# Separate accumulator banks at the projection's end, an early first step for the MLP's second product, and later due times for its weights

## The chip, the cores and the metric

The kernel runs on one core of one Trainium2 chip. The engines of the core are TensorE (PE in the rows; its weight loads are PEld), VectorE (DVE), ScalarE (ACT), GpSimd (POOL) and SyncE (SP), which only issues transfers here; ACT issues some too. The metric is the device time in microseconds (us), lower is better.

## The reference

One decoder layer over 1024 prompt tokens and 64 sample tokens: a mixing sub-layer (differential attention and sparse attention, in parallel, one output projection) and a squared-ReLU MLP, both with an RMS norm before and after.

```python
mix = jnp.concatenate([o_diff, o_nsa], axis=-1) @ w_out     # 1024 x 1024
x = x + rms_norm(mix, g_post_mix)
hm = rms_norm(x, g_pre_mlp)
ff = jnp.square(jax.nn.relu(hm @ w_up)) @ w_down            # 1024 x 4096, 4096 x 1024
x = x + rms_norm(ff, g_post_mlp)
```

Everything is fp32.

## The kernel before

Each fp32 operand is split into a high and a low part: ACT copies the high part (L139), DVE subtracts to get the low part (L1364). Three matmuls (high x high, low x high, high x low) make one fp32 product, so before PE can use a new operand it needs one ACT and one DVE instruction on it.

Four stages matter here, and they follow one another without a barrier. The program order is handed to a scheduler that works out its own time line and so decides the order on each engine; then each engine runs its rows strictly in that order, and waits where a row's input is not there.

1. **Attention.** Its last work items (score, transpose T, product o) end while the projection begins.
2. **Projection** (`phase_out`). The weights of `w_out` are loaded and split (`weight(k)`, 8 of them), and for each of nine token tiles `front(t)` loads the attention's output and splits it, `prod(t, 0)` and `prod(t, 1)` make two half rows (C, 24 matmuls of 512 columns each), and `post(t)` does norm, residual, second norm and transposes (T, 8 of them). `post` is a chain over engines: ACT (sum of squares), DVE, POOL (`rstd`), DVE (L1309, L1310), ACT, DVE, POOL, DVE (L1314), then the transposes on PE. C has 3 of the 8 accumulator banks, T has 2. `x_factor` (DVE, ACT) then builds the token side of the MLP's operands; `up_open` and `up_factor` load and build its first weight side.
3. **MLP up** (`phase_up`). One level of a seven-product scheme for a 2x2 block product (`UORD`, `DORD` give the order of the products), tiled over 16 column blocks j. The tokens are two quarters p (`QT` = 272 columns). For j = 0 the first quarter is done alone, `products(0, (0,))`, while the operands of the second quarter are still being built; then its second quarter, then the other j. The accumulators Ua to Ud take two banks each, all eight, so they can be opened only when C and T are done with theirs. Results (uh) go to hF in DRAM by SP.
4. **MLP down** (`phase_down`). 128 steps n over (product i, row block sb): each step needs a 128-row block of a quarter of `w_down` (wf, from q or qe) and a row block of hF (hf, from hr), both split by ACT and DVE; the first 96 issue 24 matmuls of 272 columns each (Dn, L1648), the last 32 half of that (L1658). The 16 steps of the first product use quarter 0 alone; its first eight blocks come in two 1 MB loads on ACT's queue into qe, the other eight into q02 and q03 on SP's. The chunks of quarters 1, 3 and 2 (q10 to q23, 1 MB each) are loaded later: a gate, a copy of one element on DVE (L1552) at step `gate` = 2, 6, 10, ..., holds each load back; DVE then combines the chunk with another one (L1566, L1568). `finish` writes result rows; `fin` gives it one of four rooms.

## Time and profile before

| what | value |
|---|---|
| three runs | 1845.38, 1856.58, 1858.5 us; median 1856.58 |
| profiled execution, its own time | 1848.67 us |
| its span | 1846.9 us (1.8 us lie around it) |
| PE busy | 1718.9 us, 93% of the span |
| projection | about 973 to 1098 us |
| MLP up | about 1107 to 1456 us |
| MLP down | about 1469 to 1834 us, then the last rows until 1846.9 |

Times in the rows are us from the start of the span. The granted clock of PE (PEclk) is a share of full speed, averaged over the stretch. Matmuls are pipelined and their ends are modelled, so a row's duration is a little more than the time until the next row.

### The profile page before, as it was taken

What the parts mean: (1) busy time and instruction counts of PE and PEld (TensorE: products, weight loads), DVE (VectorE), ACT (ScalarE), POOL (GpSimd) and SP (SyncE); (2) the same over time, 40 slices, a digit from 0 to 9 for tenths busy, and PEclk for the clock granted to TensorE, in tenths of its full rate; (3) what the DMA queues carried; (4) which work ended last, traced back from release to release, by engine and by line L of the source; (5) the groups of instructions that cost most, each with busy time, mean ns of one, the idle gap of its engine ahead of it and who ended that gap; (6) DMA issues with size and microseconds to landing.
All of it is one profiled execution on the core that took longest, in us unless ns stands there. A gap on an engine that the chain in (4) does not pass through costs nothing.

```text
span 1846.9 us, 33392 instructions
## 1 busy us (share of the span) xinstructions
PE 1718.9 (93%) x12155; PEld 1494.1 (81%) x12155; DVE 1137.5 (62%) x2713; ACT 867.2 (47%) x2188; POOL 275.8 (15%) x517
## 2 busy tenths in 40 slices
PE   7698999999998999999978978999999689999997
PEld 7677776676656877788867858999999689999996
DVE  5357657667753666667583477665766356747655
ACT  5254446556652554546462345444444234443442
POOL 2134325333320111111110010000000000000000
PEclk9888999999998999999988989999999889999999
DMA  7521000001104342433253322443443545544434
GB/s 204 111 72 43 13 11 21 7 7 42 35 8 135 107 123 67 139 89 118 74 198 100 116 84 71 138 153 138 143 145 114 213 163 171 177 119 116 114 118 140
DMA packets 193904, 191.92 MB, mean 104 GB/s; under 512 B 32547, under 2 KB 152971, under 8 KB 193739
## 3 DMA queue, kind: packets, MB, share of 16 engines
q1 hardware_dynamic: 190810, 184.30, 32.5%
q10 hardware_dynamic: 2928, 5.48, 0.9%
q8 instruction: 96, 1.57, 0.4%
q14 instruction: 70, 0.57, 0.1%
HBM read 133.75 MB, written 55.97 MB: 103 GB/s over the span
## 4 chain that ended last, share of the span: by engine, by line
PE 76%; DVE 8%; DMA 6%; issue 3%; ACT 2%; SPq 1%; POOL 1%; ACTq 0%; DVEq 0%; POOLq 0%
PE Dn L1648 12%; PE M L337 11%; PE S L410 5%; PE o L502 5%; PE Uc L1438 5%; PE Ua L1438 5%; PE Ub L1438 5%; PE T L517 4%; PE C L1294 4%; PE Dn L1658 3%; PE Ud L1438 2%; DMA q<-w_down 2%; PE o L614 2%; PE S L1097 1%; PE o L1222 1%
## 5 line engine op out<-in xcount | busy, mean ns | idle before, releaser
L1648 PE MATMUL Dn<-hf,wf 128*128 128x272 f32 x2304 | 296.7, 292 | 22.9 <-ACT hf L139 13.7
L1648 PEld LDWEIGHTS Dn<-hf,wf 128*128 128x128 f32 x2304 | 295.1, 192 | 24.4 <-ACT hf L139 14.1
L337 PE MATMUL M<-w,xt 128*128 128x384 f32 (+4 forms) x1584 | 296.1, 332 | 13.2 <-ACT natk L139 10.7
L337 PEld LDWEIGHTS M<-w,xt 128*128 128x128 f32 (+1 forms) x1584 | 246.0, 192 | 28.5 <-ACT natk L139 11.5
L427 ACT ACTIVATE p<-S,nm 128x512 f32<-128x512 f32 (+3 forms) x288 | 160.2, 562 | 87.4 <-DVE nm L422 47.2
L175 POOL TENSOR_TENSOR rs_r<-rs_t,mhalf 128x1 f32<-128x1 f32 (+2 forms) x64 | 39.7, 621 | 983.1 <-DVE rs_t L173 980.1
L418 DVE TENSOR_REDUCE nm<-S 128x1 f32<-128x512 f32 (+3 forms) x288 | 148.2, 528 | 58.0 <-PE S L417 37.8
L410 PE MATMUL S<-kst,qs 128*128 128x512 f32 (+3 forms) x576 | 162.5, 373 | 9.0 <-ACT p L427 8.2
L481 POOL TENSOR_SCALAR p<-p,coef 128x640 f32<-128x640 f32 (+7 forms) x128 | 92.9, 739 | 150.2 <-DVE coef L478 66.3
L410 PEld LDWEIGHTS S<-kst,qs 128*128 128x128 f32 x576 | 94.1, 194 | 22.1 <-ACT p L427 11.4
L1364 DVE TENSOR_TENSOR us<-ur,us 128x512 fp32r<-128x512 f32 x96 | 65.9, 691 | 66.5 <-ACT us L139 66.5
L1438 PE MATMUL Ub<-xc,us 128*128 128x272 f32 x768 | 105.7, 290 | 0.8 <-ACT us L139 0.8
L1438 PE MATMUL Ua<-xc,us 128*128 128x272 f32 x768 | 103.4, 290 | 2.3 <-ACT uh L139 2.3
L139 ACT ACTIVATE wf<-q 128x512 fp32r<-128x512 f32 x72 | 45.7, 635 | 125.9 <-PE Dn L1648 118.4
L139 ACT ACTIVATE us<-ur 128x512 fp32r<-128x512 f32 x101 | 63.3, 629 | 83.3 <-PE Uc L1438 50.2
L1438 PEld LDWEIGHTS Ua<-xc,us 128*128 128x128 f32 x768 | 99.6, 190 | 2.6 <-ACT uh L139 2.5
L1438 PEld LDWEIGHTS Ub<-xc,us 128*128 128x128 f32 x768 | 100.6, 190 | 1.1 <-ACT us L139 1.0
L150 DVE COPY pt<-T 128x512 f32<-128x512 f32 (+3 forms) x100 | 61.8, 619 | 55.3 <-PE T L517 41.5
L139 ACT ACTIVATE hf<-hr 128x544 fp32r<-128x544 f32 (+1 forms) x128 | 75.6, 591 | 43.0 <-PE Dn L1658 29.2
L1364 DVE TENSOR_TENSOR hf<-hr,hf 128x544 fp32r<-128x544 f32 (+1 forms) x128 | 82.7, 649 | 19.8 <-ACT hf L139 19.6
L139 ACT ACTIVATE pt<-T 128x512 f32<-128x512 f32 (+4 forms) x116 | 60.8, 527 | 68.9 <-PE T L517 41.1
L1364 DVE TENSOR_TENSOR wf<-q,wf 128x512 fp32r<-128x512 f32 x72 | 49.8, 691 | 69.7 <-ACT wf L139 69.7
(340 smaller groups left out, 3336.9 us busy)
## 6 DMA issues: line engine op xcount, KB each, us to landing
hF<-uh SPq DMA_DIRECT2D x105, 272.0 KB
hr<-hF SPq DMA_DIRECT2D x92, 272.0 KB
kvp<-cache_diff_kv SPq DMA_DIRECT2D x128, 128.0 KB
ur<-w_up SPq DMA_DIRECT2D x32, 512.0 KB
q<-w_down SPq DMA_DIRECT2D x14, 1024.0 KB
raw<-w_in SPq DMA_DIRECT2D x32, 192.0 KB
raw<-w_in SPq DMA_DIRECT2D x40, 128.0 KB
hr<-hF SPq DMA_DIRECT2D x32, 136.0 KB
```

The source lines that it names most:

```text
L139: self.nc.scalar.activation(out, in_, AF.Copy, scale=scale)
L337: nc.tensor.matmul(ps[1][:m, :n], self.xt[c][:, a, k, c0:c0 + m], ws[k][:, b, :n], start=i == 0, stop=i == len(ops) - 1)
L410: nc.tensor.matmul(S[:, a * P - lo:b * P - lo], qs[:, ps, j, :], kst[hf][:, kc, a * P - lo:b * P - lo], start=ps == 0, stop=ps == 1 and no ...
L418: nc.vector.reduce_max(nm[:, n:n + 1], S[:, a * P - lo:b * P - lo], axis=AX.X, negate=True)
L427: nc.scalar.activation(p[:, a * P:b * P], tiles[n][:, a * P - lo:b * P - lo], AF.Exp, bias=nm[:, 0:1], accum_out=sums[:, n:n + 1])
L481: nc.gpsimd.tensor_scalar(v, v, coef[:, sw + 1, j:j + 1], 0.0, op0=OP.mult, op1=OP.add)
L502: nc.tensor.matmul(st["o"][half * 64:half * 64 + 64, pr * 256:pr * 256 + 256], lhsT, rhs, start=not started[half], stop=last, skip_group_c ...
L517: nc.tensor.transpose(T[:, m * 256 + jj * P:m * 256 + jj * P + P], st["p", sw, pr * 2 + jj][:, kb * P:(kb + 1) * P], self.ident)
L1294: nc.tensor.matmul(ps[:m], mhs[t][:, a, k, :m], ws[k][n][:, b], start=cnt == 0, stop=cnt == 3 * KC - 1)
L1364: lo.tensor_sub(w[:, 1], src, f32(w[:, 0]))
L1438: nc.tensor.matmul(ps[:, p, :QT], w[:, a, k, :], x[:, b, k, :], start=start and cnt == 0, stop=cnt == 11, skip_group_check=True)
L1648: nc.tensor.matmul(dps[db][:, q, :QT], w[:, a, db * P:(db + 1) * P], h[:, b, q * QT:(q + 1) * QT], start=st and m == 0, stop=sp and m == 2)
```

## The change

In `phase_out`, `front(0)` stands ahead of all weights, and the opening of the MLP's first weights stands between tile 7 and tile 8 of the second half rows. The first quarter of j = 0 gets banks of its own, one each (Va to Vd, pool `psU0`), open from the start of the projection; T keeps one bank, and U is opened when the first quarter is done. `down_open` loads block 0 of `w_down`'s quarter 0 (eq) and row block 0 of the first product of hF (eh0) while MLP up runs. The rest of quarter 0 is cut into blocks 1 to 4 and 5 to 8 (qe, ACT's queue), 9 to 12 (q03) and 13 to 15 (q04, both SP). The gates of the later chunks stand at 6, 10, 14, ... in place of 2, 6, 10, ...; `fin` has three rooms; uh has 12 buffers, not 13, and some pools lie elsewhere.

```diff
@@ -1265,10 +1265,8 @@
             nc.vector.tensor_sub(mh[:, 1, :, :m], mx[:, :, :m], f32(mh[:, 0, :, :m]))
             pss[t] = []
 
-        for k in range(2):
-            weight(k)
         front(0)
-        for k in range(2, KC):
+        for k in range(KC):
             weight(k)
         for i in UORD[:5]:
             self.xtile(self.xca, i, 0)
...
@@ -1343,12 +1341,13 @@
         for t in range(NT - 1, NT + 1):
             front(t)
             prod(t, 0)
-        self.up_open()
-        for i in UORD[:5]:
-            self.up_factor(0, i)
         for t in range(NT - 1, NT + 1):
             prod(t, 1)
             post(t)
+            if t < NT:
+                self.up_open()
+                for i in UORD[:5]:
+                    self.up_factor(0, i)
...
@@ -1439,15 +1438,16 @@
...
-        def products(j, pq, nxt, st=lambda: self.sp.tile([P, 2, QT], F32, name="uh", bufs=13)):
...
             def ptile(x):
-                if pq[0] == 0:
-                    self.ups[x] = psU.tile([P, 2, 512], F32, name=f"U{x}", tag=f"U{x}")
-                t = self.ups[x]
+                if pq == (0,):
+                    t = self.psU0.tile([P, 1, 512], F32, name=f"V{x}", tag=f"V{x}")
+                else:
+                    t = self.psU.tile([P, 2, 512], F32, name=f"U{x}", tag=f"U{x}")
                 return t, t[:, s, :QT]
...
         turn = iter(UORD)
-        products(0, (0,), lambda i: self.x_factor(next(turn), 1), lambda: self.sp.tile([P, 1, QT], F32, name="uh", bufs=13))
+        products(0, (0,), lambda i: self.x_factor(next(turn), 1), lambda: self.sp.tile([P, 1, QT], F32, name="uh", bufs=12))
         close(1)
         for j in range(NJ):
             if j + 2 < NJ:
                 load(j + 2)
+            if j == NJ - 2:
+                self.down_open()
             products(j, (0, 1) if j else (1,), lambda i: factor(j + 1, i))
+
+    def down_open(self):
+
+        nc = self.nc
+        self.eq = self.early.tile([P, 1, 512], F32, name="eq")
+        nc.sync.dma_start(self.eq, self.A["w_down"][0].rearrange("(s e p) c -> e p s c", e=2, p=P)[0, :, 0:1, 0:512])
+        self.eh = []
+        for sb in range(1):
+            h = self.early.tile([P, HT], F32, name=f"eh{sb}")
+            nc.sync.dma_start(h, self.hF[DORD[0], sb * P:sb * P + P])
+            self.eh.append(h)
...
         def load_w(q, c, gate=None):
-            early = q == 0 and c < 2
-            t = quarter[q, c] = (qe if early else qp).tile([P, 4, 512], F32, name="qe" if early else f"q{q}{c}",
-                                                           bufs=2 if early else 1)
+
+            r, e = q % 2, q // 2
+            s0, s1 = (max(c * 4 - 3, 0), min(c * 4 + 1, NB)) if q == 0 else (c * 4, c * 4 + 4)
+            if q == 0 and c == 0:
+                t = self.eq
+            elif q == 0 and c < 3:
+                t = qe.tile([P, 4, 512], F32, name="qe", bufs=2)
+            else:
+                t = qp.tile([P, s1 - s0, 512], F32, name=f"q{q}{c}")
             if gate is not None:
                 nc.vector.tensor_copy(t[:, 0, 0:1], gate)
-            r, e = q % 2, q // 2
-            (nc.scalar if early else nc.sync).dma_start(t, w_dn[e, :, c * 4:c * 4 + 4, r * 512:r * 512 + 512])
+            for sb in range(s0, s1):
+                quarter[q, sb] = t[:, sb - s0]
+            if (q, c) != (0, 0):
+                (nc.scalar if q == 0 and c < 3 else nc.sync).dma_start(t, w_dn[e, :, s0:s1, r * 512:r * 512 + 512])
 
 
         def factor(n):
             if n >= len(hr):
                 return
             i, sb, p = hr[n]
-            load_h(n + HB)
-            a11, a21, a12, a22 = ((quarter[q, sb // 4][:, sb % 4] if (q, sb // 4) in quarter else None)
-                                  for q in range(4))
+            load_h(n + 4)
+            a11, a21, a12, a22 = (quarter.get((q, sb)) for q in range(4))
...
         def fin(n):
 
-            if n < 4:
-                room[n] = None
-            if room[n % 4] is None or n >= 4:
-                room[n % 4] = qe.tile([P, 4, 512], F32, name="qe", bufs=2) if n % 4 < 2 else \
-                    qp.tile([P, 4, 512], F32, name=f"q0{n % 4}")
-            return room[n % 4]
-
-        room = {}
+            return qp.tile([P, 4, 512], F32, name="q03") if n % 3 == 2 else qe.tile([P, 4, 512], F32, name="qe", bufs=2)
+
         gate = {}
         for k, (q, c) in enumerate([(q, c) for q in (1, 3, 2) for c in range(4)]):
-            gate[2 + (k % 4) * 4 + (k // 4) * NB] = (q, c)
-        for c in range(4):
+            gate[6 + (k % 4) * 4 + (k // 4) * NB] = (q, c)
+        R.update(enumerate(self.eh))
+        for c in range(5):
             load_w(0, c)
-            load_h(c, nc.scalar)
             if c < 2:
+                load_h(2 * c + 1, nc.scalar)
+                if c:
+                    load_h(2, nc.scalar)
                 factor(c)
...
                 self.rr = e(self.pool("rr", side="right"))
+                self.wa = e(self.pool("wa", side="right"))
                 xca = e(self.pool("xca", side="right"))
-                self.wa = e(self.pool("wa"))
...
+                up0 = e(ExitStack())
+                self.psU0 = up0.enter_context(self.pool("psU0", psum=True))
                 with self.pool("w2", 11) as self.wp, self.pool("cl") as cl, \
-                        self.pool("psC", 3, psum=True) as self.psC, self.pool("psT2", 2, psum=True) as self.psT:
+                        self.pool("psC", 3, psum=True) as self.psC, self.pool("psT2", 1, psum=True) as self.psT:
...
-                with self.pool("xcb") as xcb, self.pool("psU", psum=True) as psU:
+                early = ExitStack()
+                self.early = early.enter_context(self.pool("early"))
+                with self.pool("xcb") as xcb, ExitStack() as ps:
...
                         self.xstack[0].close()
                         if p == 1:
                             self.xstack[1].close()
+                            up0.close()
+                            self.psU = ps.enter_context(self.pool("psU", psum=True))
                         self.sp = self.xstack[0].enter_context(self.pool(f"sp{p}", side="right"))
...
+            with early, self.pool("qe", side="right") as qe, self.pool("fd") as fp, self.pool("qd") as qp, \
                     self.pool("psDn", 4, psum=True) as psD:
                 self.phase_down(qe, qp, fp, psD)
```

Three places show what this does to the order of rows. The first is PE at the end of attention (T, o) and the projection's start (C, by weights `w` and `us`). Before:

```order
L1294 MATMUL C_12910<-w_12847,xm_12815 128x512 x3
L1294 MATMUL C_12910<-w_12855,xm_12815 128x512 x3
L1294 MATMUL C_12910<-w_12863,xm_12815 128x512 x3
L1294 MATMUL C_12971<-us_12799,xm_12968 128x512
L603 MATMUL T_12728<-ident_64,p_12675 128x128 [waits Activation_49]
L603 MATMUL T_12728<-ident_64,p_12675 128x128 x3
L614 MATMUL o_12735<-vst_11344,pt_12726 128x128 [waits Activation_49]
L614 MATMUL o_12735<-vst_11344,pt_12726 128x128 x3
L1294 MATMUL C_12971<-us_12799,xm_12968 128x512 x2
L1294 MATMUL C_12971<-us_12807,xm_12968 128x512 x3
L1294 MATMUL C_12971<-us_12820,xm_12968 128x512 x3
L1294 MATMUL C_12971<-us_12828,xm_12968 128x512 x3
```

and with the change:

```order
L565 MATMUL T_12710<-ident_64,jk_12702 128x128 [waits DVE_49,PE_49]
L603 MATMUL T_12721<-ident_64,p_12675 128x128 [waits PE_49]
L603 MATMUL T_12721<-ident_64,p_12675 128x128 x3
L603 MATMUL T_12728<-ident_64,p_12675 128x128 [waits Activation_49]
L603 MATMUL T_12728<-ident_64,p_12675 128x128 x3
L614 MATMUL o_12735<-vst_11344,pt_12726 128x128 [waits Activation_49]
L614 MATMUL o_12735<-vst_11344,pt_12726 128x128 x3
L614 MATMUL o_12735<-vst_11345,pt_12733 128x128 [waits Activation_49]
L614 MATMUL o_12735<-vst_11345,pt_12733 128x128 x2
L614 MATMUL o_12735<-vst_11345,pt_12733 128x128 [waits Pool_49]
L565 MATMUL T_12754<-ident_64,jk_12746 128x128 [waits DVE_49,PE_49]
L1292 MATMUL C_12886<-us_12807,xm_12802 128x512 x3
```

Before, the last transposes and o products of attention stand between C matmuls of two tiles (72 C matmuls ahead of the last T); now all of attention is first and C follows it.

The second is PE at the projection's end; the last C rows are tile 8's second half, T_13702 are its transposes. Before:

```order
L1294 MATMUL C_13658<-w_12863,xm_13545 64x512 x3
L1319 MATMUL T_13646<-ident_64,ctmp_13627 128x128 [waits DVE_49,Activation_49]
L1319 MATMUL T_13646<-ident_64,ctmp_13627 128x128 x3
L1319 MATMUL T_13652<-ident_64,ctmp_13627 128x128 [waits Activation_49]
L1319 MATMUL T_13652<-ident_64,ctmp_13627 128x128 x3
L1319 MATMUL T_13702<-ident_64,ctmp_13683 128x64 [waits DVE_49,Activation_49]
L1319 MATMUL T_13702<-ident_64,ctmp_13683 128x64 x3
L1319 MATMUL T_13709<-ident_64,ctmp_13683 128x64 [waits Activation_49]
L1319 MATMUL T_13709<-ident_64,ctmp_13683 128x64 x3
L1438 MATMUL Ua_13751<-xc00_12866,us_13583 128x272 x12
L1438 MATMUL Ub_13768<-xc50_12867,us_13586 128x272 [waits PE_49,Activation_49]
```

and with the change (T_13503 belongs to tile 6, C_13661 is the second half of tile 8):

```order
L1437 MATMUL Va_13754<-xc00_12869,us_13642 128x272
L1317 MATMUL T_13503<-ident_64,ctmp_13478 128x128 [waits Activation_49]
L1317 MATMUL T_13503<-ident_64,ctmp_13478 128x128 x3
L1437 MATMUL Va_13754<-xc00_12869,us_13642 128x272 x6
L1437 MATMUL Vb_13771<-xc50_12870,us_13645 128x272 [waits Activation_49]
L1437 MATMUL Vb_13771<-xc50_12870,us_13645 128x272 x3
L1437 MATMUL Vb_13771<-xc50_12870,us_13645 128x272 [waits DVE_49]
L1437 MATMUL Vb_13771<-xc50_12870,us_13645 128x272 x7
L1437 MATMUL Vc_13822<-xc40_12873,us_13658 128x272 [waits Activation_49]
L1437 MATMUL Vc_13822<-xc40_12873,us_13658 128x272 x3
L1292 MATMUL C_13661<-w_12810,xm_13548 64x512 [waits DVE_49]
L1292 MATMUL C_13661<-w_12810,xm_13548 64x512 x2
```

Va, Vb and the beginning of Vc now stand ahead of the last 24 C matmuls; the transposes of tiles 7 and 8 follow after them and eight more matmuls of Vc, and Vd follows the transposes.

The third is the change from MLP up to MLP down, on ACT (L1554 and L1574 are loads of weights, L1545 and L1557 those of hF; L1462 and L1463 are MLP up's last squared ReLU). Before:

```order
L1463 ACTIVATE uh_17450<-uh_17450 128x544 [waits Activation_49]
L1554 DMA qe_17568<-w_down 128x4x512 [waits DMAHW7_49,PE_49]
L1554 DMA qe_17580<-w_down 128x4x512 [waits DMAHW0_49]
L1462 ACTIVATE uh_17396<-uh_17396 128x544 [waits DMAHW6_49,DMAHW2_49,DVE_49]
L1463 ACTIVATE uh_17396<-uh_17396 128x544 [waits Activation_49]
L139 ACTIVATE wf_17574<-qe_17568 128x512 [waits DMAHW7_49]
L139 ACTIVATE wf_17586<-qe_17568 128x512
L139 ACTIVATE wf_17608<-qe_17568 128x512
L1545 DMA hr_17570<-hF_60 128x544 [waits DMAHW5_49]
```

and with the change:

```order
L139 ACTIVATE wf_17587<-eq_17123 128x512
L139 ACTIVATE hf_17590<-eh0_17125 128x544
L1463 ACTIVATE uh_17465<-uh_17465 128x544 [waits Activation_49]
L1574 DMA qe_17593<-w_down 128x4x512 [waits DMAHW0_49]
L1574 DMA qe_17607<-w_down 128x4x512 [waits DMAHW1_49]
L1462 ACTIVATE uh_17411<-uh_17411 128x544 [waits DMAHW5_49,DMAHW2_49,DVE_49]
L1463 ACTIVATE uh_17411<-uh_17411 128x544 [waits Activation_49]
L139 ACTIVATE wf_17601<-qe_17593 128x512 [waits DMAHW0_49]
L139 ACTIVATE wf_17621<-qe_17593 128x512
L139 ACTIVATE wf_17657<-qe_17593 128x512 [waits PE_49]
L1557 DMA hr_17583<-hF_60 128x544 [waits DMAHW7_49]
```

The splits of step 0 (wf from eq, hf from eh0) now stand ahead of the two loads of qe; step 1's hF load stands where step 0's stood. On DVE, the gate of q10 and its first use, before (wf and hf are the splits of steps 0 to 3):

```order
L1364 TENSOR_TENSOR wf_17608<-qe_17568,wf_17608 128x512 [waits Activation_49]
L1552 COPY q10_17674<-wf_17608 128x1 [waits DVE_49]
L1364 TENSOR_TENSOR hf_17577<-hr_17570,hf_17577 128x544 [waits DMAHW5_49,Activation_49]
L1364 TENSOR_TENSOR hf_17589<-hr_17582,hf_17589 128x544 [waits DMAHW0_49,Activation_49]
L1364 TENSOR_TENSOR wf_17644<-qe_17568,wf_17644 128x512 [waits Activation_49]
L1566 TENSOR_TENSOR qe_17568<-qe_17568,q10_17674 128x512 [waits DMAHW4_49,DVE_49]
L1566 TENSOR_TENSOR qe_17568<-qe_17568,q10_17674 128x512 x2
L1566 TENSOR_TENSOR qe_17568<-qe_17568,q10_17674 128x512 [waits DVE_49]
```

and with the change (splits of steps 6 to 8):

```order
L1363 TENSOR_TENSOR hf_17756<-hr_17619,hf_17756 128x544 [waits DMAHW7_49,Activation_49]
L1570 COPY q10_17815<-wf_17753 128x1 [waits DMAHW5_49,DVE_49]
L1363 TENSOR_TENSOR wf_17785<-qe_17607,wf_17785 128x512 [waits Activation_49]
L1363 TENSOR_TENSOR hf_17788<-hr_17655,hf_17788 128x544 [waits DMAHW0_49,Activation_49]
L1363 TENSOR_TENSOR wf_17820<-qe_17607,wf_17820 128x512 [waits Activation_49]
L1363 TENSOR_TENSOR hf_17823<-hr_17687,hf_17823 128x544 [waits DMAHW1_49,Activation_49]
L1585 TENSOR_TENSOR eq_17123<-eq_17123,q10_17815 128x512 [waits DMAHW4_49,DVE_49]
L1585 TENSOR_TENSOR qe_17593<-qe_17593,q10_17815 128x512 x3
```

The gate's copy and the subtraction moved from steps 0 and 2 to steps 6 and 8; two steps lie between them in both.

## Rows read from the trace of the kernel before

**Rows 1.** The page: busy time of PE, and the chain that ended last
```profile
PE 1718.9 (93%) x12155; PEld 1494.1 (81%) x12155; DVE 1137.5 (62%) x2713; ACT 867.2 (47%) x2188; POOL 275.8 (15%) x517
...
PE 76%; DVE 8%; DMA 6%; issue 3%; ACT 2%; SPq 1%; POOL 1%; ACTq 0%; DVEq 0%; POOLq 0%
```

**Rows 2.** Stretches: length, busy us and instructions by engine, PEclk, DMA share, GB/s
```profile
960.00:980.00 20.00, 16.83 (x72) 13.55 (x71) 11.29 (x26) 10.33 (x29) 2.21 (x2) 0.77 0.58 183
980.00:1000.00 20.00, 14.85 (x74) 11.99 (x73) 4.68 (x8) 5.32 (x15) 1.10 (x2) 0.92 0.27 86
1080.00:1100.00 20.00, 14.44 (x59) 9.28 (x58) 13.60 (x22) 8.76 (x18) 1.46 (x3) 0.83 0.23 78
1100.00:1120.00 20.00, 13.62 (x89) 13.54 (x90) 17.00 (x19) 10.33 (x18) 0.72 (x2) 0.74 0.09 22
...
1460.00:1480.00 20.00, 9.83 (x56) 9.61 (x56) 6.07 (x10) 5.43 (x10) 0.00 (x0) 0.66 1.04 382
```

**Rows 3.** PE in order of time at the switch: start, us, what, [idle before, releaser]
```profile
1454.83 1.66 PE L1438 MATMUL Uc<-xm,us 128*128 128x272 f32 x12
1468.90 8.79 PE L1648 MATMUL Dn<-hf,wf 128*128 128x272 f32 x48 [12.41 <-ACT hf L139]
1478.95 1.27 PE L1648 MATMUL Dn<-hf,wf 128*128 128x272 f32 x8 [1.27 <-ACT hf L139]
1486.88 5.37 PE L1648 MATMUL Dn<-hf,wf 128*128 128x272 f32 x24 [6.66 <-DVE hf L1364]
...
1504.73 25.47 PE L1648 MATMUL Dn<-hf,wf 128*128 128x272 f32 x202
```

**Rows 4.** ACT in order of time at the switch (ACTq: issue of transfers)
```profile
1456.53 1.00 ACTq L1554 DMA_DIRECT2D qe<-w_down  x2
...
1462.00 0.63 ACT L139 ACTIVATE wf<-qe 128x512 fp32r<-128x512 f32 x1 [3.00 <-DMA qe<-w_down]
1462.01 0.35 ACTq L1545 DMA_DIRECT2D hr<-hF  x1
...
1468.19 0.66 ACT L139 ACTIVATE hf<-hr 128x544 fp32r<-128x544 f32 x1 [4.52 <-DMA hr<-hF]
```

**Rows 5.** SP and DVE in order of time at the switch
```profile
1467.97 1.19 SPq L1554 DMA_DIRECT2D q<-w_down  x2
...
1483.09 2.50 DVE L1566 TENSOR_TENSOR qe<-qe,q 128x512 f32<-128x512 f32 x4 [7.01 <-DMA q<-w_down]
```

**Rows 6.** MLP down: who waited for whom (total, times, longest), and PE's row
```profile
DVE q L1568 <- DMA q<-w_down: 8.1, 3, 3.6
...
1575.36 14.91 PE L1648 MATMUL Dn<-hf,wf 128*128 128x272 f32 x102 [1.75 <-DVE wf L1364]
```

**Rows 7.** PE in order of time inside and at the end of the projection
```profile
1046.83 7.86 PE L1294 MATMUL C<-w,xm 128*128 128x512 f32 x33
...
1090.14 8.27 PE L1294 MATMUL C<-w,xm 128*64 128x512 f32 x24 [4.84 <-DVE ctmp L1309]
1098.25 1.03 PE L1319 MATMUL T<-ident,ctmp 128*128 128x128 f32 x8
1106.38 1.08 PE L1319 MATMUL T<-ident,ctmp 64*128 64x64 f32 x8 [7.09 <-DVE ctmp L1314]
1107.39 3.09 PE L1438 MATMUL Ua<-xc,us 128*128 128x272 f32 x12
```

**Rows 8.** The stretch after the projection: columns as in the second group
```profile
1106.00:1128.00 22.00, 17.85 (x116) 17.04 (x116) 21.18 (x25) 13.90 (x22) 0.00 (x0) 0.85 0.04 13
```

**Rows 9.** PE in order of time at the projection's start
```profile
972.83 3.75 PE L1294 MATMUL C<-us,xm 128*128 128x512 f32 x15
...
994.20 0.30 PE L565 MATMUL T<-ident,jk 128*128 128x128 f32 x1 [1.55 <-DVE jk L563]
998.10 6.20 PE L1294 MATMUL C<-w,xm 128*128 128x512 f32 x15 [3.60 <-DVE ctmp L1309]
```

**Rows 10.** C's matmuls alone in the same stretch: length, PE, PEld, PEclk, DMA share, GB/s
```profile
972.00:994.20 22.20, 17.79 (x72) 13.23 (x72) 0.98 0.15 48
```

**Rows 11.** The last stretch: columns as in the second group
```profile
1834.00:1847.00 13.00, 0.39 (x4) 0.11 (x2) 7.43 (x9) 3.10 (x6) 2.52 (x3) 0.72 0.24 91
```

More of the change, by code (lines that the diff above doesn't have):

```diff
@@ L1424, in up_open, with phase_up @@
         load(1)
-    def phase_up(self, psU, close):
+    def phase_up(self, close):
         nc = self.nc
```

5 lines of the change are left out of this document (2 added, 3 removed).

## Prediction

> **What bounds the kernel now.** The page first: PE is busy 93% of the span and makes 76% of the chain that ended last [rows 1]. So PE sets the time, and a change can only give back time in which PE stands still or runs slowly. The table of stretches shows where that is: the reader is to look at PE's busy column and at PEclk together. Three places stand out [rows 2]: the projection's start (16.83 and 14.85 of 20 us busy), its end (14.44 and 13.62, clock 0.83 and 0.74), and the switch from MLP up to MLP down (9.83, clock 0.66). They are the three places that the change touches. For each, PE's rows in order of time give the wait and what ended it. A change within 1% (18.6 us) is about what a measurement of this kernel can't tell from no change.
>
> **The switch from MLP up to MLP down.** The last Uc matmuls end at 1454.83 + 1.66 = 1456.49; the first Dn starts at 1468.90 after 12.41 us [rows 3]. ACT's rows show why: the loads of qe are issued at 1456.53, the first lands 5.5 us later at 1462.00, only behind it does ACT's queue issue step 0's hF load (1462.01), and that lands 6.2 us later at 1468.19 [rows 4]. Then 48 matmuls take 8.79 us, 1.27 us of waiting, 8 matmuls, another wait of 6.66, and 24 matmuls in 5.37, until 1492.25 [rows 3]. Dense, 202 matmuls take 25.47, so 0.126 each and 3.03 a step [rows 3]. By 1492.25 there are 80 done, worth 10.1 us; 35.8 have gone by, so 25.7 are lost. The second wait comes from DVE: its in-order queue held q10's subtraction for 7.01 us, since q10 was issued after 1467.97 and landed only at 1483.09, 15 us later, with the transfer engines full (DMA share 1.04, 382 GB/s) [rows 2, 5].
>
> With the change, step 0's operands are on the chip before MLP up ends, and its splits stand ahead of the last ones of MLP up. They are two instructions of about 0.7 on ACT and two on DVE [rows 4], ahead of the last additions and under the last Uc matmuls. So step 0 follows Uc directly and dense: 1456.5 to 1459.5. Step 1 then hangs on the chain on which step 0 hung: qe, then an hF load behind it on ACT's queue. With the same two latencies it starts at 1468.9, so PE waits 9.4. Its clock will have fallen, as it had after the 12.41 before: I take the same 48 matmuls in 8.79, 2.7 over dense. After that nothing holds DVE, because q10's gate and subtraction stand at steps 6 and 8, when the first quarter's traffic is through. Two steps, 6.1 us, lie between them, as for all twelve chunks before and after; three of these already made DVE wait 8.1 in all at L1568, for which PE paid 1.75 in the largest case [rows 6]. I allow 1 us for q10. Lost: 9.4 + 2.7 + 1 = 13.1, against 25.7: **a gain of 12.5**. The upper bound is 15, if step 1's load lands at once after qe's two (DVE and PE then start some 2 us earlier). The lower bound is 8: by 1463 the new order has asked for (by the tiles' shapes) 2.1 MB of qe, 1.8 of q03 and q04, three hF loads of 0.28, the norm's 0.5 and MLP up's last four stores, 1.1; these 6.3 MB at 382 GB/s [rows 2] take 16.5, so if step 1's load is the last of them it lands near 1473 in place of 1468.2, and 4 to 5 of the gain are gone. The Trainium skill, page "DMA: Bandwidth & Descriptors", section "Issuing engines are not separate DMA queues", says that transfers of ACT, SP and GpSimd run on the same 16 engines and interleave, so a second queue gives no priority. By that rule the sum would stand nearer to 8 than to 12.5; the trace doesn't contradict it, as 6.2 us for 272 KB are long. I keep 12.5, because step 0's load before had much the same company and took those 6.2.
>
> The other eleven gates come four steps later, with unchanged distance to their use, and all are needed at the earliest 16 steps after the chunk they replace. So mid-down I count nothing, with 4 us each way for where the stalls of [rows 6] fall. Three rooms in place of four touch only the last tiles, which end behind DVE and ACT work [rows 11]; the third room's earlier store has ended by then: 0, at most +1.
>
> **The projection's end.** PE waits 4.84 for a C bank (DVE's L1309), runs tile 8's 24 matmuls in 8.27, waits 7.09 for post(8)'s chain, and starts U at 1107.39 [rows 7]. Dense, 33 C matmuls take 7.86 [rows 7], so 24 take 5.7: the low clock cost 2.6. That is 14.5 in all. With own banks, Va, Vb and Vc fill these waits. But they only move PE's work forward. The work behind is DVE's: the token operands of both quarters and the first weights, in one queue with post's steps. DVE is busy 21.18 of the 22 us behind the projection [rows 8], and the second quarter of j = 0 can't start until it is through, whatever PE did meanwhile; U's banks overlie V's, so it waits for the first quarter's readers as well. PE can gain only what DVE was idle for: 6.4 in 1080 to 1100 and 3.0 in 1100 to 1120 [rows 2], 9.4 at most, and most of that is post's alternation of ACT, DVE and POOL, which stays; the transposes of tile 8 now even queue behind C and V on PE. The other bound: thinly spread PE work runs at the low clock for one more tile, a loss of 2.6. I take **a gain of 2**, nearer to the lower end, as the row nearest to it, DVE's 21.18 of 22, shows that engine full.
>
> The single T bank makes each tile's transposes two halves with an eviction between. 24 C matmuls (5.7 us) lie around them and hide it in tiles 0 to 6; if that cover were gone, half a transpose group (0.5 us) a tile would show. Counted at nothing.
>
> **The projection's start.** Before, C begins at 972.83, and its matmuls fill the waits of attention's tail, up to the last transpose at 994.20; then PE waits 3.60 for post(0) [rows 9]. C's 72 matmuls take 17.79 of those 22.2 us [rows 10]. With the change attention's tail runs alone and C follows it without a break. Without C in between, the tail can be faster: PE's own work in it is 22.2 - 17.8 = 4.4, and its ACT and DVE links (splits and transposes of two heads) come to about as much again, so C begins some 8 later, near 981. The 72 matmuls then take 72 x 0.238 = 17.1 dense, until 998.1, just where the next C matmul started before: the 3.60 for post(0) is covered, since two tiles' halves lie between. The weights' splits behind front(0) cost nothing as long as attention's tail covers them; without that cover the 16 low parts would show on DVE, 0.7 each. After the thin tail the first tile runs at the low clock, 2.6 as above for 24 matmuls. I take **a loss of 2**. Bounds: -4, if the tail needs only its 4.4 and C ends its 72 near 994.3; +13.5, if the last transpose comes at 994.20 as before and all 17.1 of C lie behind it, less the 3.6.
>
> **Sum.** -12.5 - 2 + 2 = -12.5. The profiled execution took 1848.67, so its like would be 1836.2. The median of the three runs lies 7.9 above the profile, and nothing says which level the next runs take; I put the change on the median: 1856.6 - 12.5 = **1844**.
>
> **Rivals.**
> *The projection's end is freed.* If DVE's queue can take post(7) and post(8) earlier because V's products let it start their evictions early, all of 9.4 and 2.6 come back in place of 2: 10 more, 1834. For it speak DVE's idle 9.4, against it DVE's 21.18 of 22.
> *The loads interleave.* Step 1's load shares its engines with all that is asked for at once: the gain at the switch is 8 or less, the sum -8, 1848.5; if q10 then still holds DVE, only the early step 3.03 remains, and the sum is -3, 1853.5. DMA share 1.04 speaks for it, the earlier load's 6.2 us against it.
> *Attention's tail lies open, and the kernel is slower.* C is the filler of 960 to 1000. If the tail's links take as long without it as with it, the last transpose again comes near 994, PE loses 13.5 in place of 2, and its first tile runs at the low clock (2.6): 1844 - 2 + 13.5 + 2.6 = 1858. It decides when the last transpose comes later than about 992. Against it: before, PE's queue itself delayed that chain, with up to 18 C matmuls between two of its links.
>
> **Chances.** My forecast 0.5; its own range is 1836 to 1855 (switch 15 to 8, end -2.6 to +5, start -4 to +5). The freed end 0.2, the loads 0.17, the open tail 0.08, something else 0.05. Faster by over 1% means under 1838: nearly all of the freed end (0.19) and a third of the forecast (0.16), together 0.35. Slower by over 1% means above 1875, which none of the sums reaches; I leave 0.07 for the open tail with more stalls behind it and for the unknown. Within 1%: 0.58. The range is 1829 to 1860: the freed end below, the open tail above, and six us for the level of the runs.
>
> **What would show it.** Right at the switch: one Dn group of 24 directly behind Uc, one wait near 9 us ended by hf's split, none by q10's subtraction in the next 20 us. At the projection's end: Va to Vc between C rows, DVE busy above 0.95 until the second quarter starts, and the second Ua group of j = 1 within 3 us of where it was relative to tile 7's start. At the start: C begins near 981 and doesn't stop for post(0). Wrong: Dn waiting over 12 us for step 1; DVE waiting for q10 or q30 to q33 for more than 8.1 in all, with PE rows that follow it; PE idle over 6 us in a row while attention ends.

## The result, and the profile after

The changed kernel takes 1831.27 us (median of 4 runs, 1827.18 to 1833.78) beside 1853.87 us for the kernel before on the same chip (1845.38 to 1858.5): a ratio of 0.9881, 95% interval 0.9838 to 0.9924. It is 1.2% faster. The forecast was 1844, 0.7% faster, with 0.35 for faster by over 1%; 1831 lies in the range of 1829 to 1860, near its lower end, and below the 1836 to 1855 that the forecast had for itself. The profiled execution has a span of 1828.7 us beside 1846.9.

The page after, as in [rows 1]:

```profile
PE 1714.7 (94%) x12155; PEld 1491.8 (82%) x12155; DVE 1136.4 (62%) x2713; ACT 866.2 (47%) x2188; POOL 274.0 (15%) x517
```

PE does the same work; what went is time around it. The same stretches as in [rows 2] (length, busy us and instructions by engine, PEclk, DMA share, GB/s):

```profile
960.00:980.00 20.00, 13.05 (x58) 10.94 (x57) 12.07 (x26) 11.62 (x31) 1.99 (x2) 0.70 0.65 212
980.00:1000.00 20.00, 18.73 (x75) 15.13 (x76) 4.38 (x8) 2.75 (x7) 1.09 (x2) 0.91 0.04 8
1080.00:1100.00 20.00, 15.65 (x88) 11.90 (x86) 15.76 (x24) 9.78 (x19) 1.95 (x3) 0.96 0.28 92
1100.00:1120.00 20.00, 10.44 (x44) 8.92 (x44) 18.12 (x20) 12.24 (x19) 0.54 (x1) 0.59 0.09 21
...
1460.00:1480.00 20.00, 14.59 (x99) 14.59 (x100) 6.50 (x11) 5.47 (x10) 0.00 (x0) 0.74 0.84 302
```

PE gains in 980 to 1000 and loses in 960 to 980; at the projection's end it gains in 1080 to 1100 and loses 3 us and clock (0.59 in place of 0.74) in 1100 to 1120; at the switch it gains 4.8. PE's rows at the switch, which answer to [rows 3]:

```profile
1451.51 1.67 PE L1437 MATMUL Uc<-xm,us 128*128 128x272 f32 x12
1453.02 0.45 PE L1664 MATMUL Dn<-hf,wf 128*128 128x272 f32 x2
1453.71 3.02 PE L1664 MATMUL Dn<-hf,wf 128*128 128x272 f32 x22 [0.24 <-DVE hf L1363]
1465.41 34.79 PE L1664 MATMUL Dn<-hf,wf 128*128 128x272 f32 x258 [8.68 <-ACT hf L139]
```

Step 0 follows Uc, one wait of 8.68 is left, and 258 matmuls run behind it without a stop.

To compare executions, the three places are measured from rows of each execution itself, since what lies ahead varies: the last group of 40 products of decode attention (L1126) begins at 942.26 in the kernel before, and at 950.25 in the first experiment below, whose rows are the same up to there. "First" runs from there to the second column block's Ua (24 matmuls), "middle" to the last 12 Uc, "last" to the end of the span. Rows of before, then of after:

```profile
942.26 1.43 PE L1126 MATMUL o<-kvp,dpt 128*32 128x128 f32 x40
...
1136.75 3.17 PE L1438 MATMUL Ua<-xc,us 128*128 128x272 f32 x24
```

```profile
941.72 1.43 PE L1126 MATMUL o<-kvp,dpt 128*32 128x128 f32 x40
...
1133.35 3.18 PE L1437 MATMUL Ua<-xc,us 128*128 128x272 f32 x24
```

| kernel | first | middle | last | ratio to before (95%) |
|---|---|---|---|---|
| before | 194.5 | 318.1 | 392.1 | |
| after | 191.6 | 318.2 | 377.2 | 0.9881 (0.9838 to 0.9924) |
| gates only | 194.4 | 318.1 | 378.9 | 0.9954 (0.9931 to 0.9977) |
| gates back | 189.6 | 318.2 | 380.4 | 0.9925 (0.9903 to 0.9947) |
| MLP down only | 188.1 | 318.1 | 377.3 | 0.9898 (0.9869 to 0.9926) |
| banks only | 191.6 | 318.1 | 388.7 | 0.9979 (0.9958 to 1.0001) |
| pool's side only | 188.2 | 318.1 | 390.1 | 0.9968 (0.9946 to 0.9991) |
| C's banks first | 182.3 | 318.1 | 374.2 | 0.9834 (0.9800 to 0.9867) |
| + weights ahead | 185.3 | 318.1 | 375.5 | 0.9877 (0.9841 to 0.9913) |
| + quiet load | 185.2 | 318.1 | 375.0 | 0.9839 (0.9802 to 0.9875) |
| low parts on GpSimd | 187.8 | 318.1 | 374.7 | 0.9874 (0.9838 to 0.9910) |
| early issue | 183.9 | 318.1 | 374.2 | 0.9850 (0.9816 to 0.9883) |
| these two | 185.5 | 318.1 | 378.5 | 0.9901 (0.9866 to 0.9937) |
| norm load away | 182.3 | 318.1 | 372.9 | 0.9835 (0.9817 to 0.9854) |

Each ratio is to the kernel before on the same chip. In the row "these two" one execution of four, 2105.66 us at a granted clock of 0.739, is not counted.

Where the code of a stretch is the same, the figures still differ by up to 2.0 in "first" (after, gates back) and 3.4 in "last" (before, banks only, pool's side). So 2.9 of the 18.2 came in "first", 14.9 in "last", and 0.5 ahead of L1126's group; as averages over the kernels with the same code, 3.9 in "first" (194.4 to 190.6) and 14.5 in "last" (390.3 to 375.8, the latter of after, MLP down only, C's banks first, + weights ahead and low parts on GpSimd).

A mark inside "first" is the 336th C matmul, counted in PE's records: it starts 124.1 behind L1126's group in the kernel before and 123.5 in the changed one. The expectations below give such times about 1 us earlier (123.1 and 122.7 for these two), and the way from there to the second column block 1 us longer; this hardly changes the differences.

### The profile page after: what moved, and what is told of

It is laid out like the page before. It is cut to its first block, busy times and chain, and to the rows that moved or that the text cites. A ratio compares the mean times of both kernels' runs of the same rounds, so it can differ in the third digit from the quotient of the medians.

```text
span 1828.7 us, 33387 instructions
## 1 busy us (share of the span) xinstructions
PE 1714.7 (94%) x12155; PEld 1491.8 (82%) x12155; DVE 1136.4 (62%) x2713; ACT 866.2 (47%) x2188; POOL 274.0 (15%) x517
## 5 line engine op out<-in xcount | busy, mean ns | idle before, releaser
L1664 PE MATMUL Dn<-hf,wf 128*128 128x272 f32 x2304 | 292.7, 290 | 11.8 <-ACT hf L139 8.7
L1664 PEld LDWEIGHTS Dn<-hf,wf 128*128 128x128 f32 x2304 | 291.2, 190 | 13.2 <-ACT hf L139 8.9
L1437 PE MATMUL Ub<-xc,us 128*128 128x272 f32 x744 | 100.8, 288 | 0.0
L1437 PEld LDWEIGHTS Ub<-xc,us 128*128 128x128 f32 x744 | 96.1, 188 | 0.0
L517 PEld LDWEIGHTS T<-ident,p 128*128 128x128 f32 x528 | 56.5, 141 | 40.7 <-issue 35.0
```

Of the source, the lines that this page charges most:

```text
L517: nc.tensor.transpose(T[:, m * 256 + jj * P:m * 256 + jj * P + P], st["p", sw, pr * 2 + jj][:, kb * P:(kb + 1) * P], self.ident)
L1437: nc.tensor.matmul(ps[:, p, :QT], w[:, a, k, :], x[:, b, k, :], start=start and cnt == 0, stop=cnt == 11, skip_group_check=True)
L1664: nc.tensor.matmul(dps[db][:, q, :QT], w[:, a, db * P:(db + 1) * P], h[:, b, q * QT:(q + 1) * QT], start=st and m == 0, stop=sp and m == 2)
```

## The experiments

**The switch: which edit gives the 14.9?** Gates alone on the kernel before:

```diff
-            gate[2 + (k % 4) * 4 + (k // 4) * NB] = (q, c)
+            gate[6 + (k % 4) * 4 + (k // 4) * NB] = (q, c)
```

> The kernel before with one edit: the gates of the later weight chunks at steps 6, 10, ... in place of 2, 6, .... Nothing is loaded early, and banks and projection are as before. Theory A (most of what the switch gives comes from q10 leaving the first steps): the first Dn still waits about 12.4 us, until about 1469, but the later waits of 1.27 and 6.66 and the slow 24 matmuls after them go, so 9 to 10 us less than the kernel before (span near 1837). Theory B (the early step is what counts): the second wait only moves to another transfer of the first quarter, and the time stays within 2 us of before.

Its last stretch is 13.2 shorter than before (11.4 against the average of 390.3), somewhat more than the 9 to 10 of theory A. PE's row, and DVE's at q10:

```profile
1476.62 23.61 PE L1648 MATMUL Dn<-hf,wf 128*128 128x272 f32 x166 [12.25 <-ACT hf L139]
```

```profile
1499.74 2.50 DVE L1566 TENSOR_TENSOR qe<-qe,q 128x512 f32<-128x512 f32 x4 [0.25 <-DMA q<-w_down]
```

The first wait is still 12.25, and nothing stops PE behind it; DVE waits 0.25 for q10 where it had waited 7.01 [rows 5]. The opposite, the changed kernel with its gates at 2 again (the same line, reversed):

> The changed kernel with the gates put back to steps 2, 6, .... The early step, the banks and the projection stay changed. Theory A: step 0 still follows MLP up directly, but DVE waits again 5 to 7 us for q10 among the first steps, PE stands behind it and restarts slowly: 8 to 10 us more than the changed kernel (span near 1838). Theory B: within 2 us of the changed kernel (1829), since the early step was the gain.

It lost 3.2 in the last stretch (4.6 against the average of 375.8), between the two theories:

```profile
1469.77 12.00 PE L1664 MATMUL Dn<-hf,wf 128*128 128x272 f32 x80 [9.26 <-ACT hf L139]
1483.56 16.71 PE L1664 MATMUL Dn<-hf,wf 128*128 128x272 f32 x119 [1.79 <-DVE hf L1363]
```

```profile
1480.37 0.69 DVE L1585 TENSOR_TENSOR eq<-eq,q 128x512 f32<-128x512 f32 x1 [4.22 <-DMA q<-w_down]
```

DVE waits 4.22 for q10, but PE had 80 matmuls ready in that time (56 before) and waits only 1.79. So either edit by itself removes most of the second wait: gates 13.2, the early step with its new chunks and loads 11.7, both 14.9 (against the average of 390.3: 11.4, 9.9 and 14.5). They are not a sum.

**Do the places add up?** MLP down's changes alone, that is the changed kernel with the other parts of the diff undone:

```diff
-        front(0)
-        for k in range(KC):
+        for k in range(2):
+            weight(k)
+        front(0)
+        for k in range(2, KC):
             weight(k)
...
-                if pq == (0,):
-                    t = self.psU0.tile([P, 1, 512], F32, name=f"V{x}", tag=f"V{x}")
...
-                        self.pool("psC", 3, psum=True) as self.psC, self.pool("psT2", 1, psum=True) as self.psT:
+                        self.pool("psC", 3, psum=True) as self.psC, self.pool("psT2", 2, psum=True) as self.psT:
```

> The changes of MLP down alone (early step, chunks, gates, rooms, where its pools lie), on the projection and the banks of before. If the three places add up: C begins at 973, the first half of MLP up is where it was before (second column block at about 1136.8), and the switch gives 14 us (18.2 in all less 3.4 that stand before the switch in the changed kernel). Rival: the parts help one another, and this one alone gives under 11 or over 17.

The last stretch is as in the changed kernel, 377.3, but the first is 6.4 shorter than before, and shorter than with the whole change. This was not expected by either side: the kernel with one part of the change is ahead of the whole at the projection, and its ratio, 0.9898, can't be told from that of the whole change, 0.9881. Then the banks alone, on the kernel before:

```diff
-                if pq[0] == 0:
-                    self.ups[x] = psU.tile([P, 2, 512], F32, name=f"U{x}", tag=f"U{x}")
-                t = self.ups[x]
+                if pq == (0,):
+                    t = self.psU0.tile([P, 1, 512], F32, name=f"V{x}", tag=f"V{x}")
+                else:
+                    t = self.psU.tile([P, 2, 512], F32, name=f"U{x}", tag=f"U{x}")
...
+                up0 = e(ExitStack())
+                self.psU0 = up0.enter_context(self.pool("psU0", psum=True))
```

> Own banks for the first quarter, one T bank, and the first weights opened later, alone, on the kernel before (front(0) still stands after two weights). The order of PE's rows has C behind all of attention here too, so it is the banks and not front(0) that put it there: C begins near 981 in place of 973. Theory A: the start still comes out level or up to 2 us early because C then runs dense, the end of the projection gives 2, together 2 to 4 us by the second column block of MLP up, and nothing later. Rival: without front(0) first, C starts later than 983 and eats the gain: 0 or a loss up to 3 us.

C starts at 984.00, 39.5 behind L1126's group (984.00 - 944.51), as in the changed kernel (981.32 - 941.72 = 39.6) and not 30.6 as before. So the banks put C behind all of attention, without front(0). The gain in "first" is 2.9.

**What made the first stretch shorter with MLP down's part?** The part carries one line that the prediction hadn't spoken of: the pool of split weights lies on the other side of the memory.

```diff
+                self.wa = e(self.pool("wa", side="right"))
                 xca = e(self.pool("xca", side="right"))
-                self.wa = e(self.pool("wa"))
```

> The kernel before with one line moved: the pool wa (split weights) lies on the other side of the on-chip memory, as it does in the changed kernel; nothing else. In its order of rows post(0)'s two gain loads stand earlier on ACT's queue, and C starts earlier among attention's rows. Times counted from the start of the last group of 40 products of decode attention (L1126), because what lies before it varies by 10 us between executions of the same code. Theory: this unmentioned line is what made the start 6 us shorter in the run with MLP down's changes alone (C's 336th matmul at 116.8 in place of 123.1), so here too it comes at 116 to 118, and everything after is as in the kernel before. Rival: that came from the other pools of MLP down, and here it stays at 122 to 124.

The first stretch is 188.2, and the 336th C matmul comes at 118.1 in place of 124.1: theory confirmed, 6.3 from one line in "first". In its order post(0)'s work stands earlier on ACT's queue: the loads of its gains are issued at 948.25 and 948.63 and its first square at 986.21, between attention's last splits. In the kernel before, ACT issued the two loads only at 992.39 and 994.54 and began the squares behind them, at 994.98, and PE waited 3.60 for post(0) [rows 9]; in this run PE has no wait there. Which of the two, the loads or the squares, held post(0) was not tested; the row of its first DVE step (L1309, 997.29) names rstd, which hangs on the squares.

**Why doesn't the changed kernel have that gain?** It has that line too. The banks again: attention's scores have the first three banks and leave early, its transposes have banks that are in use to the end. Va to Vd took the early ones.

```diff
                 up0 = e(ExitStack())
+                self.psC = up0.enter_context(self.pool("psC", 3, psum=True))
+                self.psT = up0.enter_context(self.pool("psT2", 1, psum=True))
                 self.psU0 = up0.enter_context(self.pool("psU0", psum=True))
-                with self.pool("w2", 11) as self.wp, self.pool("cl") as cl, \
-                        self.pool("psC", 3, psum=True) as self.psC, self.pool("psT2", 1, psum=True) as self.psT:
+                with self.pool("w2", 11) as self.wp, self.pool("cl") as cl:
```

> The changed kernel, with the accumulator banks handed out in another order: C's three and T's one first, Va to Vd behind them. Before, C had the first three banks, which attention's scores leave early; in the changed kernel Va to Vd have them and C has banks of attention's transposes, which are in use to the end. Counted from the same group at L1126. Theory: C starts near 29 to 31 in place of 39.6, the 336th C matmul comes at 116 to 118.5 in place of 122.7, the projection's end still takes 69 from there to the second column block (before: 71.4), so 4 to 6 us less than the changed kernel in all. Rival: the start is bound by attention's own chain and by post(0), and C's early start gives less than 2.

PE's rows of this kernel:

```profile
947.00 1.43 PE L1126 MATMUL o<-kvp,dpt 128*32 128x128 f32 x40
...
976.45 4.11 PE L1292 MATMUL C<-us,xm 128*128 128x512 f32 x15
...
1129.25 3.18 PE L1437 MATMUL Ua<-xc,us 128*128 128x272 f32 x24
```

C starts at 29.5, its 336th matmul comes at 115.0, and from there to the second column block it takes 67.2. The first stretch is 9.4 shorter than in the changed kernel, more than the 4 to 6 expected. With 0.9834 it is clearly ahead of the kernel before; against the changed kernel (0.9881) the two intervals just overlap, and it is the stretches that show the gain. Beside it, with two weights ahead of front(0) as before:

```diff
+        for k in range(2):
+            weight(k)
         front(0)
-        for k in range(KC):
+        for k in range(2, KC):
             weight(k)
```

> As the run with C's banks first, but with two weights ahead of front(0), as in the kernel before; so it undoes front(0)'s move alone beside it. Theory: C stands among attention's rows as in the run of MLP down's changes alone, and the 336th C matmul comes within 1.5 us of the run with C's banks first; the move of front(0) is worth little either way. Rival: the move counts, and the two differ by over 2.

The 336th C matmul comes at 117.9 here and at 116.8 in the next run, whose code is the same up to there; with front(0) first it comes at 113.4 to 115.2, 114.6 on average, in the five kernels that share that code. So the rival holds: front(0) first is worth 2.9 in this pair and 2.7 on average, once C no longer stands behind attention.

**What ends the wait of 8.68?** The prediction had it as two transfers, one behind the other. ACT's rows of the changed kernel (ACTq: issue of transfers):

```profile
1451.82 0.39 ACTq L1574 DMA_DIRECT2D qe<-w_down  x1
...
1457.44 0.63 ACT L139 ACTIVATE wf<-qe 128x512 fp32r<-128x512 f32 x1 [1.77 <-DMA qe<-w_down]
1457.45 0.35 ACTq L1557 DMA_DIRECT2D hr<-hF  x1
...
1460.58 3.14 ACTq L1557 DMA_DIRECT2D hr<-hF  x2
1464.32 0.34 ACTq L1641 DMA_DIRECT2D gpm<-g_post_mlp  x1
1464.70 0.66 ACT L139 ACTIVATE hf<-hr 128x544 fp32r<-128x544 f32 x1 [5.59 <-DMA hF<-uh]
```

Step 1's block of hF, issued at 1457.45, landed at 1463.60 by the landing records of the trace, 6.1 later; the split began another 1.1 later, 0.4 behind the issue of gpm, the gain of the last norm. The expectation that follows took all 7.2 for the load.

Is step 1's load slow because of its company? Here all but qe's first megabyte is held back (on the kernel with weights ahead):

```diff
+        load_w(0, 0)
+        load_h(1, nc.scalar)
+        factor(0)
+        load_w(0, 1)
+        for n in (2, 3):
+            load_h(n, nc.scalar)
+        factor(1)
+        for c in (2, 3, 4):
+            load_w(0, c, gate=f32(F[1][1][:, 1, 0:1]))
```

> As the run before (C's banks first, two weights ahead of front(0)), and at the switch qe's second megabyte, q03 and q04 are held back by a gate until step 1's hF block is split; only qe's first megabyte and three hF loads share the transfer engines. Theory: step 1's hF load took 7.2 us from issue to landing in the changed kernel because of that company; here it takes 3.5 to 5, so PE's wait between steps 0 and 1 falls from 8.7 to 5 to 6.5, and no new wait appears at step 5, whose weights then have some 10 us to land: 2 to 3.5 us less. Rival: the 7 us are the transfer's own, whatever else runs: the wait stays above 8, or the weights held back make PE wait at step 5 and eat the gain.

```profile
1457.09 1.33 ACTq L1559 DMA_DIRECT2D hr<-hF  x2
...
1459.54 0.34 ACTq L1645 DMA_DIRECT2D gpm<-g_post_mlp  x1
1462.29 0.66 ACT L139 ACTIVATE hf<-hr 128x544 fp32r<-128x544 f32 x1 [3.55 <-DMA hr<-hF]
```

The load takes 5.2 here, its landing ends the wait, and gpm's issue stands 2.8 ahead of the split. PE's wait is 8.4 (9.5 in the run beside it, where the load took 6.0): 1.1 less. The company matters little; the rival came nearer. Then the order of issues: the hF loads of steps 1 to 3 from GpSimd's queue, on the kernel with C's banks first:

```diff
+        for n in (1, 2, 3):
+            load_h(n, nc.gpsimd)
         for c in range(5):
             load_w(0, c)
             if c < 2:
-                load_h(2 * c + 1, nc.scalar)
-                if c:
-                    load_h(2, nc.scalar)
                 factor(c)
```

> As the run with C's banks first, with one edit at the switch: the hF loads of steps 1 to 3 are issued from GpSimd's queue, which has nothing else to do, in place of ACT's, where they stand behind the split that waits for qe's first megabyte. Theory (the wait between steps 0 and 1 is two transfers one after the other, 5.6 and 6 to 7 us): here they overlap, step 1 starts when qe has landed and is split, and the wait falls from 8.3 to 4 to 5.5, 3 to 4 us less, with a second wait of at most 1 to 3 at step 2, whose block comes later. Rival (the transfers share the engines, so that both land later): the wait stays above 7.

```profile
L1557 POOL DMA_DIRECT2D hr<-hF x3: 548/554/740, 1443.6 to 1444.9; - x3
...
DMA to landing us min/median/max: 3.2/3.3/4.6
```

```profile
1459.24 0.35 ACTq L1640 DMA_DIRECT2D gpm<-g_post_mlp  x1
1459.63 1.75 ACT L139 ACTIVATE hf<-hr 128x544 fp32r<-128x544 f32 x3 [5.33 <-DMA hF<-uh]
```

The loads landed 3.2 to 4.6 after their issue at 1443.6 to 1444.9, and still the wait was 8.61. Neither theory holds. Both here and in the changed kernel the split of step 1 starts 0.4 behind the issue of gpm, and the row names a store of MLP up as what ended its wait. Gpm's issue comes only when those stores have landed, and ACT's rows behind it come after it. In the changed kernel that cost 1.1 beyond the load itself; here, where the blocks had landed by 1449.6, it was the whole wait. So gpm moved as well, behind the three loads on GpSimd's queue:

```diff
-        nc.scalar.dma_start(gp, A["g_post_mlp"].to_broadcast([P, D]))
+        nc.gpsimd.dma_start(gp, A["g_post_mlp"].to_broadcast([P, D]))
```

> As the run with the hF loads of steps 1 to 3 on GpSimd's queue, with one more edit: the load of the last norm's gain (gpm, 0.5 MB, needed some 350 us later) moves from ACT's queue to GpSimd's, behind those three. In that run, as in the changed kernel, ACT's split of step 1 began within 0.4 us of gpm's issue, and gpm's issue waits for MLP up's last stores; its hF loads had landed 3.3 us after their issue, ten us earlier. Theory: gpm's issue, not a transfer of step 1, ends the wait between steps 0 and 1; here ACT splits step 1 directly behind qe's three splits, the wait falls from 8.6 to 4 to 5, and nothing new waits at steps 2 and 3: 3.5 to 4.5 us less than that run in the same stretch (end of MLP up to the end). Rival: the stores' landing holds step 1 in another way too (its semaphores), or DVE's last additions do, and the wait stays above 7.

```profile
1454.66 1.67 ACT L139 ACTIVATE wf<-qe 128x512 fp32r<-128x512 f32 x3 [4.58 <-DMA qe<-w_down]
1456.24 1.74 ACT L139 ACTIVATE hf<-hr 128x544 fp32r<-128x544 f32 x3
```

```profile
1456.93 43.28 PE L1663 MATMUL Dn<-hf,wf 128*128 128x272 f32 x330 [5.78 <-ACT hf L139]
```

Step 1's split now stands directly behind qe's three splits, and the wait is 5.78 in place of 8.61: with the blocks there early, gpm's issue was what ended it. In the changed kernel the load's landing and the split were 1.1 apart, so there gpm alone could give about 1.1 (an estimate from these rows); gpm moved by itself was not run. The wait is above the 4 to 5 expected, because qe's first megabyte took 8.4 from issue to landing here (5.6 in the changed kernel). In the last stretch only 1.3 of it arrives, and the ratio, 0.9835, can't be told from that of C's banks first.

**Is DVE the bound at the projection's end?** The seven low parts of the second quarter on GpSimd:

```diff
-        self.right(q, i, self.xc[i, p], self.nc.vector, self.nc.vector, 5)
+        self.right(q, i, self.xc[i, p], self.nc.vector, self.nc.gpsimd if p else self.nc.vector, 5)
```

> As the run with C's banks first (front(0) first), with one edit at the projection's end: the seven low parts of the second quarter's token operands are subtracted on GpSimd in place of DVE. GpSimd has little else there; a 128x640 operation took it 0.74 us, so 1.2 to 1.4 for these 128x1088, much like DVE's 1.2. Theory (DVE's queue is what bounds the way from tile 7 to the second quarter): seven times 1.2, 8.4 us, leave DVE's queue, PE's wait of 4.9 at Vc goes, and from the 336th C matmul to the second column block it takes 62 to 65 us in place of 68.3: 3 to 6 us less. Rival (post's chain over ACT, DVE and GpSimd and the transposes bound it): under 1.5 us less, and the wait of 5.6 at tile 8's transposes stays.

```profile
1106.03 13.24 POOL L1363 TENSOR_TENSOR xc<-xf,xc 128x1088 fp32r<-128x1088 f32 x4 [6.89 <-ACT xc L139]
```

```profile
1113.49 3.42 DVE L1375 TENSOR_TENSOR xf<-xf 128x1088 f32<-128x1088 f32 x1
```

The stretch from the 336th C matmul became 72.9, 5.7 longer. GpSimd took 2.5 to 3.6 for each part, and DVE's additions beside them took 2.7 to 3.4 in place of 1.28. The Trainium skill, page "SBUF — State Buffer", section "SBUF: two separate sides", says that a DVE operation with two inputs in that memory and a GpSimd operation that reads it share a pair of ports as an exclusive lock. The rows agree: beside the last part a DVE sum (L1503) took 2.74, which took 0.44 in the run with C's banks first. The price of 1.2 to 1.4 was wrong by itself: its 0.74 is a mean of the profile's page over eight shapes of an operation with one input, and the shortest of the seven parts took 2.5, twice DVE's 1.2. So DVE wasn't relieved, and the run doesn't test the theory as meant. It fits it only in this: when DVE's operations grew longer, the second quarter came later. Both edits in one:

> The two edits of the two runs before in one kernel. If they touch different places: the sum of the two gains within 1.5 us, by either theory.

Beside C's banks first, its first stretch is 3.2 longer and its last 4.3. The two edits apart had made the first longer by 5.5 and 1.6 and the last by 0.5 and 0.0. So they don't add up, and there is no gain in either. PE's wait at step 1 was 10.0 here: gpm was issued 13.8 behind qe's first load, not 12.4 as in the run with early issue, and the split again began 0.4 behind it. Why the stores landed later, and where the rest of the 4.3 went, stays open.

## Why the prediction came out as it did

**The switch: right, each loss somewhat smaller than taken.** Step 0 ran directly behind Uc; the wait was 8.68 where 9.4 was worked out; the slow restart (granted clock 0.50, the lower level of 1.2 GHz, in the first 4.6 us) cost 34.79 - 258 x 0.126 = 2.3 where 2.7 was taken; and DVE did not wait for q10 at all, where 1 was allowed:

```profile
1478.84 0.15 DVE L1570 COPY q<-wf 128x1 f32<-128x1 f32 x1
...
1485.05 0.69 DVE L1585 TENSOR_TENSOR eq<-eq,q 128x512 f32<-128x512 f32 x1
```

Together 14.9 in place of 12.5 (14.5 against the average), near the upper bound of 15. The working had the right rows, but the share of the two edits was open in it, and the runs show that each alone does most of it. The chain for the 9.4 held as far as it went: qe landed 5.6 behind its issue and step 1's block 6.1 behind its own, where 5.5 and 6.2 were taken. What it left out is the issue of a load that nobody needed yet, gpm, in front of the split on ACT's queue: 1.1 in the changed kernel. In the kernel before that issue stands at 1466.69, between two of the rows of [rows 4], and held nothing, as the block landed only at 1468.17. The wait came out below 9.4 even so, because qe was issued 0.3 behind the start of the last 12 Uc (1451.82 against 1451.51), where it had been 1.7 (1456.53 against 1454.83). The rival that the loads interleave did not occur: step 1's load took no longer than step 0's had.

**The projection's end: right.** 2 was taken, and from the 336th C matmul to the second column block it is 68.1 in place of 70.4: 2.3. It repeats: 70.1 to 70.6 in the four kernels without own banks for the first quarter, 67.1 to 69.3 in the eight with them (the two with low parts on GpSimd aside). Va to Vc stand between C's rows, and then PE waits elsewhere:

```profile
1087.86 5.79 PE L1292 MATMUL C<-w,xm 128*64 128x512 f32 x24
...
1102.61 0.66 PE L1317 MATMUL T<-ident,ctmp 64*128 64x64 f32 x4 [5.59 <-DVE ctmp L1312]
...
1120.39 3.09 PE L1437 MATMUL Vc<-xc,us 128*128 128x272 f32 x12 [4.27 <-DVE uh L1486]
```

The 24 C matmuls run at the full 2.4 GHz (5.79 at a granted clock of 1.00; 8.27 at 0.66 before), the wait of 4.84 is gone and that of 7.09 is 5.59, but 4.27 at Vc is new, and V's products there run at the low level (3.09 for 12, granted clock 0.50). That DVE's queue is the bound was argued and is not shown: DVE was busy 18.12 of 20 us in 1100 to 1120, below the 0.95 that was to show it, and the one run on it failed to relieve DVE.

**The projection's start: right in the row, wrong in the sign.** C began at 981.32 where 981 was worked out, and the 73rd C matmul came at 999.7, 1.6 behind the 998.1 of before. But a loss of 2 was counted, and the start was level: 0.6 gained by the 336th C matmul. The step that failed is the term behind the 3.60 wait. Before, the 24 matmuls after it took 8.30, at a granted clock of 0.67:

```profile
998.10 8.30 PE L1294 MATMUL C<-w,xm 128*128 128x512 f32 x24 [3.60 <-DVE ctmp L1309]
```

The prediction gave back the wait and not this restart, 2.6, though [rows 9] shows 15 matmuls in 6.20; it counted the low clock only against the change. The rival of the open tail, with the last transpose after 992, did not occur (981.27).

**What it did not see at all** is the order of the banks. C moved behind attention because Va to Vd had taken the banks that come free first, and this hid the gain of two other lines, the pool's side (6.0 at the 336th C matmul) and front(0) first (2.7). The order of rows showed that C had moved; the cause was not looked for, and the move was priced as if it had to be. With C's banks first the start gives 9.1 (124.1 to 115.0) in place of 0.6.

**The number: partly luck.** By stretches the change gave 14.9 + 2.3 + 0.6 = 17.8, where 12.5 + 2 - 2 = 12.5 was summed. By the medians it gave 22.6; the rest is the level of the runs. The result lies below the forecast's own 1836 to 1855, and inside the whole range only through the part that stood for the freed end and for that level. The freed end, which was to give 12 and carried 0.19 of the 0.35 for over 1%, did not occur.

## What to carry to other kernels

When a change hands out memory or banks, ask which earlier owner each new tile follows, and when that one is done: here the order of three lines in which pools are opened was worth 9.4 us, beside the 18.2 of the change. Ahead of an operand that somebody waits for, every issue in the same in-order queue counts, even of a load that is needed 350 us later, if it waits for something itself. Price a wait together with the slow restart behind it, on both sides of the comparison.

## What the runs showed that was not expected

- Executions whose rows are the same up to L1126's last group reach it at 942.26 and 950.25 (before, gates only) and between 944.53 and 949.11 (the five kernels with C's banks and front(0) first), so up to 8 us of spread lie ahead of the changed places; differences of a few us were read from stretches that start behind it.
- A load's issue on ACT's queue held ACT's splits for 5 us (from 1454.3 to 1459.24 in the run with early issue), while the data it did not depend on had landed 10 us before.
- GpSimd's subtraction of 128x1088 took 2.5 to 3.6 us and stretched DVE's operations beside it from 1.28 to as much as 3.42.
- qe's first megabyte took 5.6 us from issue to landing in the changed kernel, and 6.0 and 8.4 in two variants that moved other loads (held back, early hF blocks with gpm away).
